# The way out in two halves, the gMLP half among the last latents, and 24 sums on GpSimd

## The chip, the cores and the metric

One core of a Trainium2 chip runs the whole layer. The metric is device time in microseconds, the median of the runs. Engines by the profile's names: PE is TensorE, DVE VectorE, ACT ScalarE, POOL GpSimd, SP SyncE (which issues DMAs).

## The reference

A residual layer on x of 1024 rows (tokens) by 1024 columns, float32: a half-step feed-forward network (FFN1), a mixer, FFN2, and a norm.

```python
x = x + 0.5 * swiglu(rmsnorm(x, ffn1_norm), w_gate1, w_up1, w_down1)      # hidden width 2816
h = rmsnorm(x, mix_norm) @ w_in      # u 512 | v 512 | c_q 256 | c_kv 128 | k_rope 32
y_a = gmlp_mixer(u, v, ...)          # gelu(u) * (masked 128x128 mix of rmsnorm(gelu(v)) + b): 512 wide
y_b = mla_mixer(c_q, c_kv, k_rope, ...)   # 8 heads, block-causal softmax attention: 8 * 64 = 512 wide
y = concatenate([rmsnorm(y_a, gmlp_out_norm), rmsnorm(y_b, mla_out_norm)])
x = x + y @ w_out                    # 1024 x 1024
x = x + 0.5 * swiglu(rmsnorm(x, ffn2_norm), w_gate2, w_up2, w_down2)
x = rmsnorm(x, final_norm)
```

`y @ w_out` can be taken as two products, `y_a`'s 512 columns by the first 512 rows of `w_out` and `y_b`'s by the other 512.

## The kernel before

All tensors are cut into 8 row tiles of 128 tokens. Every matmul operand is split into a high part (rounded on ScalarE or GpSimd) and a low part (the rest, by a subtraction), and a product is three matmuls: high by high, high by low, low by high.

The kernel is written as a list of steps. A step carries the work that ends in its matmuls, and `before(n, work)` puts the preparation (loads, splits, sums) n steps earlier. The list is recorded once without emitting anything, to place every tile in one SBUF ring and in the eight PSUM banks by its first and last use; then it is emitted, and a scheduler puts the instructions of each engine in a row. A tile that takes the place of another waits for the last reader of it.

The stages, in the order of the list:

- FFN1 (and FFN2 alike, tag a and b). Class `GateUp` takes gate and up weights in 11 blocks u of 256 columns. A block is loaded as two tiles `raw0`, `raw1` by four DMAs of 512 KB, and seen as quarters A11, A21, A12, A22, of which `sums` (line 443) makes S1 = A21 + A22, S2 = S1 − A11, S4 = A12 − S2 and S3 = A11 − A21 by `sum` (439), line 441, on VectorE. `split` (455 and 456) makes the high part on ScalarE and the low part on VectorE. Seven products of a block (24 matmuls each, line 468) follow. The first products, P1 and P2, of blocks 0 to 2 stand ahead of all others (`EARLY`), since they need no sums. Class `Down` then multiplies by the down weights and adds to x; its result goes to DRAM as `x1d`.
- The mixer. `v_tile`, `u_tile`, `mix_pair` and `gmlp_pair` make the gMLP's y_a; `gmlp_pair` writes each normalised row tile `ya` to DRAM as `yAd` (line 897). `latent_in` (a), `key_rope` (k), `latent_T` (c) and `latent_tile` (l) make queries, keys and values of a row tile; a latent tile is 18 matmuls (917 to 926), then squares, sums and reciprocal roots on VectorE in some 30 short operations, and the normalised `qn` and `kn`.
- Attention by items (head h, pair of query tiles pi). `head_T` (973) transposes `qn` and `kn` of one head and half of the tokens; `score_pair` (988 to 994) makes scores, their maximum on VectorE and p on ScalarE; `transposed_p` (1017, 291), `weighted` (1026, 1027) and `folded` (1038, 1040) follow some steps later. A string of letters (1082) sets in which order latents and the first five attention steps x0 to x4 alternate.
- The way out. `load_out` (from 1117) loads one block k of 128 rows of `w_out`, its high part `woh` by ScalarE (1123) and its low part `wol` by GpSimd (1124), all eight in the last steps of attention. `y_tile` reads `yAd` back, normalises y_b beside it and transposes the eight blocks of a row tile. `out_tile` (1149) multiplies by 48 matmuls (1157, 1158, 1160), adds x from `x1d` (1163), stores `x2d`, and norms and transposes the row for FFN2 (287 square, 271 power on GpSimd, 305 scaling, 300 transposes).
- FFN2, whose first weight blocks are loaded at steps named by `load_at`, and the final norm.

Of the kernel before, what the change touches and what calls it, by code (L numbers as in the profile page):

```python
# [234 lines left out]
def block(nc, x, positions, ffn1_norm, ffn1_w_gate, ffn1_w_up,  # L235
# [881 lines left out]
    def load_out(k):
        hi = tile_([P, D], f"woh{k}", F32R)
        lo = tile_([P, D], f"wol{k}", F32R)
        for e in range(2):  # L1120
            es = slice(e * 512, (e + 1) * 512)
            raw = load(tile_([P, 512], f"raw_wo{k}_{e}"), wov[:, k, es])
            nc.scalar.copy(hi[:, es], raw)
            nc.gpsimd.tensor_tensor(lo[:, es], raw, f(hi[:, es]), op=ALU.subtract)
        wo[k] = (hi, lo)
# [8 lines left out]
    def y_tile(t):  # L1134
        y = tile_([P, D], f"y{t}")
        load(y[:, 0:GW], yAd[rows(t), :])
        ysrc = mx["yB"][t // 4][:, t % 4].rearrange("p h d -> p (h d)")
        r = row_rstd(ysrc, y[:, GW:], f"yb{t}", GW)
        nc.vector.scalar_tensor_tensor(y[:, GW:], ysrc, r, mx["goB"], op0=ALU.mult, op1=ALU.mult)
        hv = transposed(y, f"y{t}")  # L1140
        yh = tile_([P, KD, P], f"yh{t}", F32R)
        yl = tile_([P, KD, P], f"yl{t}", F32R)
        for k in range(2):
            split(hv[k], yh[:, 4 * k:4 * k + 4, :], yl[:, 4 * k:4 * k + 4, :])
        mx["y", t] = (yh, yl)
# [3 lines left out]
    def out_tile(t):  # L1149
        x2 = row_tile(x1d[rows(t), :], f"x2_{t}")  # L1150
        yh, yl = mx["y", t]
        pe = [bank(f"wo{t}_{e}") for e in range(2)]
        for k in range(KD):
            wh, wl = wo[k]
            for e in range(2):
                es = slice(e * 512, (e + 1) * 512)
                mm(pe[e], yh[:, k, :], wh[:, es], start=k == 0, stop=False)  # L1157
                mm(pe[e], yh[:, k, :], wl[:, es], start=False, stop=False)  # L1158
            for e in range(2):
# [81 lines left out]
```

## Time and profile before

| | us |
|---|---|
| median of 3 runs | 1762.07 (1761.93 to 1762.74) |
| the profiled execution | 1762.42 |
| its span | 1760.6 |
| TensorE busy | 1716.5 (97%), 8196 instructions |
| VectorE busy | 1132.8 (64%) |
| ScalarE busy | 740.3 (42%) |
| GpSimd busy | 151.5 (9%) |

The busy share is an average over stages: TensorE is busy without a break in most of the two FFNs, and idle for some microseconds at a time elsewhere. A matmul counts as busy also while it runs at the lower clock, so the granted clock of a stretch is read beside its busy time.

### The profile page before, as it was taken

The numbers are of one execution on the slowest core, as the hardware profiler recorded it, in microseconds if no ns is written. First come the engines' busy times: TensorE is split into PE (matmuls) and PEld (weight loads), VectorE is DVE, ScalarE is ACT, GpSimd is POOL, SyncE is SP. The second block draws the span as 40 slices with busy tenths as digits, with TensorE's granted clock in tenths as the row PEclk, the third lists the DMA queues.
The fourth block names the chain that finished last, engine by engine and source line by source line (L and its number), as shares of the span: only waits on it lengthen the run. The fifth ranks groups of instructions, "written<-read, shape, count | busy, mean of one in ns | idle before, by whom it ended". The sixth has DMA issues, their size and how long they took to land.

```text
span 1760.6 us, 21281 instructions
## 1 busy us (share of the span) xinstructions
PE 1716.5 (97%) x8196; PEld 1446.7 (82%) x8196; DVE 1132.8 (64%) x1597; ACT 740.3 (42%) x1125; POOL 151.5 (9%) x288
## 2 busy tenths in 40 slices
PE   8999999999999999999799999999999999999997
PEld 7788888888888888898699888778888888888886
DVE  7965656555578567469777644675665555648774
ACT  6533333334324344346577823443333333433442
POOL 1100000000000004333200511000000000000010
PEclk9999999999999999999799999999999999999999
DMA  7043232325835521200000422413322231693431
GB/s 257 12 144 120 90 120 90 112 74 195 313 125 186 167 85 48 94 25 1 1 1 1 158 88 97 161 54 112 127 102 90 96 118 70 210 345 107 161 126 48
DMA packets 122981, 199.51 MB, mean 113 GB/s; under 512 B 11008, under 2 KB 57600, under 8 KB 122880
## 3 DMA queue, kind: packets, MB, share of 16 engines
q1 hardware_dynamic: 118784, 184.52, 31.1%
q0 software_dynamic: 3520, 12.58, 1.8%
q8 instruction: 64, 1.05, 0.2%
q10 hardware_dynamic: 576, 1.05, 0.2%
q14 instruction: 37, 0.30, 0.1%
HBM read 143.07 MB, written 55.05 MB: 113 GB/s over the span
## 4 chain that ended last, share of the span: by engine, by line
PE 90%; DVE 4%; ACT 3%; DMA 2%; issue 1%; POOL 0%; SPq 0%; POOLq 0%; ACTq 0%; DVEq 0%
PE psum L468 46%; PE psum L597 8%; PE psum L599 8%; PE psum L600 8%; PE psum L744 2%; PE psum L745 2%; PE psum L746 2%; PE psum L1160 2%; PE psum L1157 2%; PE psum L1158 2%; PE psum L1017 2%; PE psum L300 1%; PE psum L1027 1%; PE psum L1026 1%; PE psum L988 1%; PE psum L990 1%
## 5 line engine op out<-in xcount | busy, mean ns | idle before, releaser
L483 DVE TENSOR_TENSOR P_a<-psum,P_a 128x1024 f32<-128x1024 f32 x33 | 40.3, 1222 | 80.1 <-PE psum L468 80.1
L483 DVE TENSOR_TENSOR P_b<-psum,P_b 128x1024 f32<-128x1024 f32 x33 | 40.3, 1222 | 59.4 <-PE psum L468 59.4
L473 ACT COPY P_b<-psum 128x1024 f32<-128x1024 f32 x33 | 33.5, 1014 | 77.3 <-PE psum L468 77.3
L473 ACT COPY P_a<-psum 128x1024 f32<-128x1024 f32 x33 | 33.5, 1016 | 73.4 <-PE psum L468 73.4
L484 ACT ACTIVATE P_a<-P_a 128x512 f32<-128x512 f32 x33 | 20.9, 633 | 102.7 <-DVE P_a L483 102.6
L271 POOL TENSOR_TENSOR r_fin<-ms_fin,mhalf 128x1 f32<-128x1 f32 x8 | 7.0, 876 | 610.7 <-DVE ms_fin L269 610.7
L291 DVE TENSOR_TENSOR pl<-psum,ph 128x512 fp32r<-128x512 f32 (+1 forms) x80 | 48.5, 629 | 14.1 <-ACT ph L291 14.1
L992 DVE TENSOR_REDUCE nm<-psum 128x1 f32<-128x128 f32 (+3 forms) x64 | 47.0, 751 | 12.9 <-PE psum L990 12.8
L725 POOL DMA_DIRECT2D x1d<-x_a x8 | 4.6, 580 | 569.9 <-DVE x_a L611 568.3
L994 ACT ACTIVATE p<-psum,nm 128x128 f32<-128x128 f32 (+3 forms) x64 | 47.8, 752 | 12.9 <-DVE nm L992 11.7
L484 ACT ACTIVATE P_b<-P_b 128x512 f32<-128x512 f32 x33 | 20.8, 631 | 76.6 <-DVE P_b L483 76.4
L1157 PE MATMUL psum<-woh,yh 128*128 128x512 f32 x128 | 51.2, 400 | 0.0
L1158 PE MATMUL psum<-wol,yh 128*128 128x512 f32 x128 | 49.9, 390 | 0.0
L1017 PE MATMUL psum<-ident,p 128*128 128x128 f32 x288 | 44.2, 285 | 4.9 <-ACT p L994 4.9
L1027 PE MATMUL psum<-pl,vv 128*128 128x256 f32 x160 | 43.7, 299 | 3.2 <-DVE pl L291 3.2
L1160 PE MATMUL psum<-woh,yl 128*128 128x512 f32 x128 | 45.2, 392 | 0.0
L1026 PE MATMUL psum<-ph,vv 128*128 128x256 f32 x160 | 43.9, 298 | 1.3 <-ACT ph L291 1.3
L291 ACT CAST ph<-psum 128x512 fp32r<-128x512 f32 (+1 forms) x80 | 41.4, 559 | 8.5 <-PE psum L1017 6.6
L988 PE MATMUL psum<-kh,qh 128*128 128x512 f32 (+2 forms) x96 | 38.6, 406 | 3.7 <-ACT kn L940 3.5
L1017 PEld LDWEIGHTS psum<-ident,p 128*128 128x128 f32 x288 | 35.0, 148 | 7.7 <-ACT p L994 5.9
L611 DVE SCALAR_TENSOR_TENSOR x_b<-psum,x_b 128x512 f32<-128x512 f32 x32 | 21.0, 685 | 27.0 <-PE psum L600 27.0
L1027 PEld LDWEIGHTS psum<-pl,vv 128*128 128x128 f32 x160 | 31.3, 196 | 4.9 <-DVE pl L291 3.6
(525 smaller groups left out, 5256.9 us busy)
## 6 DMA issues: line engine op xcount, KB each, us to landing
raw_a<-in_ffn_w_gate SPq DMA_DIRECT2D x22, 512.0 KB, 4.3
raw_a<-in_ffn_w_up SPq DMA_DIRECT2D x22, 512.0 KB, 5.7
hd<-hS_a SPq DMA_DIRECT2D x44, 256.0 KB, 2.2
raw_b<-in_ffn_w_gate SPq DMA_DIRECT2D x22, 512.0 KB, 4.1
...
```

Source lines behind the costliest of these rows:

```text
L291: return nc.scalar.copy(hi, src), nc.vector.tensor_tensor(lo, src, f(hi), op=ALU.subtract)
L468: mm(bk[:, m * 512:(m + 1) * 512], lhs[:, 4 * m + k, :], rhs[:, k, :], start=pn in FIRST and n == k == 0, stop=n == 2 and k == 3, skip_gro ...
L473: nc.scalar.copy(ev[u, pn], bk)
L483: nc.vector.tensor_tensor(c, bk, c, op=ALU.add)
L597: mm(banks[t], hh[:, j, tl], dh[:, j, :], start=pn in DOWN_FIRST and c == 0 and j == 0, stop=False, skip_group_check=True)
L599: mm(banks[t], hh[:, j, tl], dl[:, j, :], start=False, stop=False, skip_group_check=True)
L600: mm(banks[t], hl[:, j, tl], dh[:, j, :], start=False, stop=c == 5, skip_group_check=True)
L1017: nc.tensor.transpose(ps[:, i * P:(i + 1) * P], prs[j][:, c * P:(c + 1) * P], ident)
L1027: mm(acc[:, 0:256], mx["vv"][c][:, h, :], lo, start=False, stop=i == len(pts) - 1)
L1157: mm(pe[e], yh[:, k, :], wh[:, es], start=k == 0, stop=False)
L1158: mm(pe[e], yh[:, k, :], wl[:, es], start=False, stop=False)
L1160: mm(pe[e], yl[:, k, :], wh[:, e * 512:(e + 1) * 512], start=False, stop=k == KD - 1)
```

## The change

Five edits, as the diff has them.

1. The way out is split by the rows of `w_out`. The normalised gMLP tiles `ya` stay in SBUF; `yAd` is gone. `load_out` of blocks 0 to 3 moves to the latents, and a new work `o` (`out_a`) takes one row tile's 24 matmuls of the gMLP half, adds x1 and stores x15 = x1 + y_a half to `x15d` by GpSimd's queue. The eight o-steps stand among the last latents and the first attention steps in the string of letters, each with its four transposes (`y_a`) a step earlier. At the end `out_tile` has the other 24 matmuls and adds to x15. The matmuls of a tile run high by high, high by low, low by high over all blocks, no longer block by block. Only `load_out` of blocks 4 to 7 is left in attention's last steps.
2. The string of letters also has another order of a, k, c and l, and only x0 to x2 in it; the attention's first rounds go over two heads where there were three, with `head_T` placed to match.
3. `sum` is on GpSimd for u < 3: 12 sums of 128x1024 in each FFN.
4. FFN2's weights of blocks 0 and 1 are loaded two steps earlier (block 1: one or two).
5. `y_tile` of tiles 2 to 7 stands two steps ahead of its out tile, not one.

Over the whole program GpSimd gets 24 sums of 128x1024 that VectorE had; VectorE gets 16 more additions of 128x512 (the gMLP half's). The number of matmuls and of ScalarE's instructions is the same.

```diff
@@ sum
-            nc.vector.tensor_tensor(t, self.value(u, x0), self.value(u, x1), op=op)
+            (nc.gpsimd if u < 3 else nc.vector).tensor_tensor(t, self.value(u, x0), self.value(u, x1), op=op)
@@ gmlp_pair
-            nc.gpsimd.dma_start(yAd[rows(t), :], ya)
+            mx["ya", t] = ya
@@ attention
-    items = [(h, pi) for ps in ((0, 1), (2, 3)) for h in range(3) for pi in ps]
-    items += [(h, pi) for h in range(3, H) for pi in range(NT // 2)]
+    items = [(h, pi) for ps in ((0, 1), (2, 3)) for h in range(2) for pi in ps]
+    items += [(h, pi) for h in range(2, H) for pi in range(NT // 2)]
...
-        if n == 2:
-            st.do(lambda: head_T(2, 0))
-        if n == 5:
+        if n == 3:
             st.do(lambda: head_T(0, 1))
             st.do(lambda: head_T(1, 1))
...
-                if op == "T" and n == 8:
-                    st.do(lambda: head_T(2, 1))
-                if op == "T" and 1 < h < H - 1 and pi in TP:
+                if op == "T" and 0 < h < H - 1 and pi in TP:
@@ the way out
+    def y_transposed(y, t, half):
+        ps = bank(f"ty{half}{t}")
+        for k in range(4):
+            nc.tensor.transpose(ps[:, k * P:(k + 1) * P], y[:, k * P:(k + 1) * P], ident)
+        yhl = tile_([P, 2, 4, P], f"yhl{half}{t}", F32R)
+        split(ps.rearrange("p (k t) -> p k t", k=4), yhl[:, 0], yhl[:, 1])
+        return yhl
+
+    def out_half(t, half, src):
+        xt = row_tile(src[rows(t), :], f"x{half}_{t}")
+        yhl = mx.pop(("yhl", half, t))
+        pe = [bank(f"wo{half}{t}_{e}") for e in range(2)]
+        for n, (i, j) in enumerate(((0, 0), (0, 1), (1, 0))):
+            for e in range(2):
+                for k in range(4):
+                    mm(pe[e], yhl[:, i, k, :], wo[4 * half + k][j][:, e * 512:(e + 1) * 512], start=n == k == 0,
+                       stop=n == 2 and k == 3)
+        for e in range(2):
+            es = slice(e * 512, (e + 1) * 512)
+            nc.vector.tensor_tensor(xt[:, es], pe[e], xt[:, es], op=ALU.add)
+        return xt
+
+    def out_a(t):
+        xt = out_half(t, 0, x1d)
+        nc.gpsimd.dma_start(x15d[rows(t), :], xt)
+
+    def y_a(t):
+        mx["yhl", 0, t] = y_transposed(mx.pop(("ya", t)), t, 0)
...
-    for ch in ("u0 u1 m0 g0 u2 u3 m1 g1 u4 u5 m2 g2 u6 u7 m3 g3 a0 c0 a1 k0 l0 c1 a2 l1 c2 a3 k1 l2 c3 a4 l3 c4 a5 k2 l4 "
-               "c5 a6 c6 a7 l5 c7 k3 x0 l6 x1 l7 x2 x3 x4").split():
+    for ch in ("u0 u1 m0 g0 u2 u3 m1 g1 u4 u5 m2 g2 u6 u7 m3 g3 a0 c0 a1 k0 l0 c1 a2 a3 k1 l1 c2 a4 a5 k2 l2 c3 a6 a7 k3 l3 c4 "
+               "o0 l4 c5 o1 l5 c6 o2 l6 c7 o3 l7 o4 x0 o5 o6 x1 o7 x2").split():
...
+    for t in range(NT):
+        sm[f"o{t}"].before(1, lambda t=t: y_a(t))
+    for k in range(4):
+        sm["o0"].before(8 - 2 * k, lambda k=k: load_out(k))
...
-    for k in range(KD):
-        att[last - 3 + k // 2].before(0, lambda k=k: load_out(k))
+    for k in range(4):
+        att[last - 2 + k // 2].before(0, lambda k=k: load_out(4 + k))
...
     def y_tile(t):
-        y = tile_([P, D], f"y{t}")
-        load(y[:, 0:GW], yAd[rows(t), :])
+        y = tile_([P, GW], f"y{t}")
...
+        mx["yhl", 1, t] = y_transposed(y, t, 1)
...
     def out_tile(t):
-        x2 = row_tile(x1d[rows(t), :], f"x2_{t}")
...
+        x2 = out_half(t, 1, x15d)
...
-        ws_[t].before(1, lambda t=t: y_tile(t), ws_[0].index)
+        ws_[t].before(2, lambda t=t: y_tile(t), ws_[0].index)
...
-    gu2.steps(GU_ORDER, base2 - 1, load_at={(0, 0): base2 - 2, (0, 1): base2 - 1, (1, 0): base2, (1, 1): base2,
+    gu2.steps(GU_ORDER, base2 - 1, load_at={(0, 0): base2 - 4, (0, 1): base2 - 3, (1, 0): base2 - 2, (1, 1): base2 - 1,
                                              (2, 0): base2, (2, 1): base2})
```

How the rows of an engine stand now, at three places. First TensorE where the last latents end: `chl6` is the transposed latent of row tile 6, `wuq`, `wkv` are its weights, `qn` and `kn` what the heads are transposed from. Before:

```order
L973 MATMUL psum_70<-ident_71,qn3_7165 128x128
L903 MATMUL psum_70<-ident_71,at1_6515 128x128 x3
L917 MATMUL psum_70<-wuq0h_6596,chl6_7409 128x384
L918 MATMUL psum_70<-wuq0l_6597,chl6_7409 128x384
L973 MATMUL psum_70<-ident_71,kn0_6785 128x128
L973 MATMUL psum_70<-ident_71,kn1_6909 128x128
L973 MATMUL psum_70<-ident_71,kn2_7043 128x128
L973 MATMUL psum_70<-ident_71,kn3_7168 128x128
L919 MATMUL psum_70<-wuq0h_6596,chl6_7409 128x384
L917 MATMUL psum_70<-wuq1h_6600,chl6_7409 128x384
L918 MATMUL psum_70<-wuq1l_6601,chl6_7409 128x384
L919 MATMUL psum_70<-wuq1h_6600,chl6_7409 128x384
```

After, behind the last six matmuls of latent 6:

```order
L924 MATMUL psum_70<-wkv_h_6599,chl6_7666 128x512
L925 MATMUL psum_70<-wkv_l_6600,chl6_7666 128x512
L926 MATMUL psum_70<-wkv_h_6599,chl6_7666 128x512
L924 MATMUL psum_70<-wkv_h_6599,chl6_7666 128x512
L925 MATMUL psum_70<-wkv_l_6600,chl6_7666 128x512
L926 MATMUL psum_70<-wkv_h_6599,chl6_7666 128x512
L1091 MATMUL psum_70<-ident_71,ya3_6373 128x128 x4
L1104 MATMUL psum_70<-woh0_7102,yhl02_7659 128x512
L1104 MATMUL psum_70<-woh1_7196,yhl02_7659 128x512
L1104 MATMUL psum_70<-woh2_7263,yhl02_7659 128x512
L1104 MATMUL psum_70<-woh3_7329,yhl02_7659 128x512
L1104 MATMUL psum_70<-wol0_7104,yhl02_7659 128x512
```

Where the kernel before went from a latent to the first head's transposes (`kn0` to `kn3`, of tiles 0 to 3) and back, the gMLP tile 3's transposes and the out tile 2's matmuls stand now.

Second, ScalarE ahead of p of head 6, row tile 6 (`p6_6`), with the copies of `w_out`'s blocks (`woh`). Before:

```order
L1123 CAST woh0_9735<-raw_wo0_0_9739 128x512
L1123 CAST woh0_9735<-raw_wo0_1_9743 128x512
L977 ACTIVATE qh7_9625<-psum_70,gqcol_95 128x512
L1123 CAST woh1_9749<-raw_wo1_0_9752 128x512
L1123 CAST woh1_9749<-raw_wo1_1_9758 128x512
L1123 CAST woh3_9849<-raw_wo3_0_9854 128x512
L977 ACTIVATE kh7_9629<-psum_70,gkcol_96 128x512
L1123 CAST woh2_9836<-raw_wo2_0_9840 128x512
L1123 CAST woh2_9836<-raw_wo2_1_9844 128x512
L1123 CAST woh3_9849<-raw_wo3_1_9858 128x512
L994 ACTIVATE p6_6_9691,rs6_3_9680<-psum_70,nm6_6_9687 128x896
```

After:

```order
L1083 CAST woh4_10166<-raw_wo4_0_10171 128x512
L1083 CAST woh4_10166<-raw_wo4_1_10176 128x512
L1083 CAST woh5_10181<-raw_wo5_0_10186 128x512
L977 ACTIVATE kh7_9988<-psum_70,gkcol_96 128x512
L1083 CAST woh5_10181<-raw_wo5_1_10191 128x512
L994 ACTIVATE p6_6_10049,rs6_3_10039<-psum_70,nm6_6_10046 128x896
L1029 COPY oT6_1_10084<-psum_70 128x256
L1083 CAST woh6_10282<-raw_wo6_0_10287 128x512
```

Eight copies of half a block stood ahead of `p6_6`; four stand there now, of blocks 4 and 5 alone.

Third, GpSimd at the start of FFN1, from the head gains (`gkcol`) on; `inv`, `posf` and `ang` belong to the rotary tables. Before:

```order
L699 TENSOR_SCALAR gqcol_95<-graw_644 64x1
L700 COPY gkcol_96<-graw_644 64x1
L704 MEMSET inv_651 128x1 x16
L706 CAST posf_669<-pos_91 128x8
L708 TENSOR_TENSOR ang_673<-posf_669,inv_651 128x128
L725 DMA x1d_86<-x_a0_3905 128x1024
```

After:

```order
L699 TENSOR_SCALAR gqcol_95<-graw_644 64x1
L700 COPY gkcol_96<-graw_644 64x1
L441 TENSOR_TENSOR S1_a0_555<-raw0_a0_117,raw1_a0_121 128x1024
L441 TENSOR_TENSOR S2_a0_558<-S1_a0_555,raw0_a0_117 128x1024
L441 TENSOR_TENSOR S4_a0_591<-raw1_a0_121,S2_a0_558 128x1024
L441 TENSOR_TENSOR S3_a0_594<-raw0_a0_117 128x1024
L704 MEMSET inv_651 128x1 x16
L706 CAST posf_669<-pos_91 128x8
L708 TENSOR_TENSOR ang_673<-posf_669,inv_651 128x128
L441 TENSOR_TENSOR S1_a1_846<-raw0_a1_320,raw1_a1_325 128x1024
L441 TENSOR_TENSOR S3_a1_885<-raw0_a1_320 128x1024
L441 TENSOR_TENSOR S2_a1_850<-S1_a1_846,raw0_a1_320 128x1024
L441 TENSOR_TENSOR S4_a1_882<-raw1_a1_325,S2_a1_850 128x1024
```

The first block's four sums stand between `gkcol` and the rotary tables, the second block's four behind these.

## Rows read from the trace of the kernel before

**Rows 1.** Stretches of the span (us): busy time (instructions) by engine, granted clock, DMA.

```profile
core 0: us, PE busy (x) PEld busy (x) DVE busy (x) ACT busy (x) POOL busy (x), PEclk, DMA share, GB/s
...
35.00:100.00 65.00, 62.46 (x278) 50.35 (x277) 57.41 (x75) 31.28 (x39) 8.03 (x20) 1.00 0.15 53
...
800.00:880.00 80.00, 65.59 (x351) 59.02 (x350) 65.06 (x196) 47.41 (x110) 24.91 (x55) 0.81 0.00 1
880.00:975.00 95.00, 93.67 (x702) 87.88 (x701) 74.28 (x143) 68.92 (x160) 6.94 (x38) 1.00 0.03 9
975.00:1000.00 25.00, 21.61 (x148) 20.07 (x147) 15.51 (x31) 22.97 (x53) 21.39 (x25) 0.93 0.50 159
1000.00:1110.00 110.00, 109.92 (x582) 93.32 (x581) 54.72 (x96) 41.54 (x85) 12.55 (x23) 1.00 0.32 108
1110.00:1170.00 60.00, 54.63 (x234) 44.45 (x233) 44.39 (x45) 28.59 (x33) 1.14 (x2) 0.94 0.30 101
```

**Rows 2.** TensorE's waits, 800–880 us: line, who ended them, sum, times, longest.

```profile
PE psum L973 <- DVE chl L291: 3.8, 1, 3.8
PE psum L988 <- ACT kn L940: 3.5, 1, 3.5
PE psum L1027 <- DVE pl L291: 3.0, 2, 2.6
```

**Rows 3.** TensorE's waits, 975–1170 us.

```profile
PE psum L468 <- ACT A11h_b L455: 3.4, 1, 3.4
PE psum L1017 <- ACT p L994: 3.2, 1, 3.2
PE psum L468 <- DVE P_b L483: 1.9, 1, 1.9
```

**Rows 4.** TensorE's timeline in the out stage: start, us, line, operation.

```profile
1043.65 0.39 PE L1157 MATMUL psum<-woh,yh 128*128 128x512 f32 x1
1043.87 0.39 PE L1158 MATMUL psum<-wol,yh 128*128 128x512 f32 x1
...
1046.37 1.04 PE L300 MATMUL psum<-ident,xn_f 128*128 128x128 f32 x8
1047.24 0.60 PE L300 MATMUL psum<-ident,y 128*128 128x128 f32 x4
```

**Rows 5.** Groups of instructions, 1020–1110 us: count | busy, mean ns | idle before.

```profile
L1163 DVE TENSOR_TENSOR x<-psum,x 128x512 f32<-128x512 f32 x14 | 9.1, 685 | 6.6 <-PE psum L1160 5.6 <-DMA x<-x1d 1.1
L305 DVE SCALAR_TENSOR_TENSOR xn_f<-x,r_f,g 128x1024 f32<-128x1024 f32 x7 | 9.0, 1285 | 5.2 <-POOL r_f L271 5.2
L291 DVE TENSOR_TENSOR yl<-psum,yh 128x512 fp32r<-128x512 f32 x12 | 8.1, 682 | 0.0
L287 ACT ACTIVATE xn_f<-x 128x1024 f32<-128x1024 f32 x7 | 7.4, 1061 | 12.0 <-DVE x L1163 9.8 <-issue 2.1
...
L271 POOL TENSOR_TENSOR r_f<-ms_f,mhalf 128x1 f32<-128x1 f32 x7 | 3.9, 559 | 4.9 <-DVE ms_f L269 4.9
```

**Rows 6.** GpSimd's groups over the whole span.

```profile
L1124 POOL TENSOR_TENSOR wol<-raw_wo,woh 128x512 fp32r<-128x512 f32 x16 | 20.2, 1312 | 1.7 <-ACT woh L1123 1.7
```

**Rows 7.** ScalarE's timeline at the end of attention.

```profile
977.63 1.20 ACT L1123 CAST woh<-raw_wo 128x512 fp32r<-128x512 f32 x2
...
982.09 1.64 ACT L1123 CAST woh<-raw_wo 128x512 fp32r<-128x512 f32 x3
983.64 1.00 ACT L994 ACTIVATE p<-psum,nm 128x896 f32<-128x896 f32 x1
```

**Rows 8.** SyncE's DMA queue before FFN2.

```profile
1109.18 0.37 SPq L311 DMA_DIRECT2D raw_b<-in_ffn_w_gate  x1
...
1115.52 1.32 SPq L311 DMA_DIRECT2D raw_b<-in_ffn_w_up  x1
```

**Rows 9.** ScalarE's timeline at the start of FFN2.

```profile
1125.98 1.04 ACT L455 CAST A11h_b<-raw_b 128x1024 fp32r<-128x1024 f32 x1 [0.34 <-DMA raw_b<-in_ffn_w_up]
```

**Rows 10.** Line 441 over the whole span: ns min/median/max.

```profile
L441 DVE TENSOR_TENSOR S_a<-raw_a,raw_a x11: 1211/1219/1226, 41.5 to 388.9; 128x1024 f32<-128x1024 f32 x11
```

**Rows 11.** GpSimd's timeline in the first 20 us.

```profile
13.85 1.04 POOL L455 CAST A11h_a<-raw_a 128x1024 fp32r<-128x1024 f32 x1
```

**Rows 12.** VectorE's timeline in the first 20 us.

```profile
13.93 2.04 DVE L305 SCALAR_TENSOR_TENSOR xn_f<-xa,r_f,g 128x1024 f32<-128x1024 f32 x1
```

**Rows 13.** GpSimd's timeline at the start of FFN1.

```profile
37.03 1.65 POOL L700 COPY gkcol<-graw 64x1 f32<-64x1 f32 x1 [0.37 <-DMA graw<-in_k_head_norm]
47.97 0.54 POOL L704 MEMSET inv<- 128x1 f32 x16 [9.29 <-DVE S_a L441]
```

More of the change, by code (lines that the diff above doesn't have):

```diff
@@ L636, in block @@
     x2d = nc.dram([S, D], "x2d")
-    yAd = nc.dram([S, GW], "yAd")
+    x15d = nc.dram([S, D], "x15d")
     hds = [nc.dram([7 * NU * P, 512], f"hd{i}") for i in range(2)]
@@ L1076, in attend, with load_out @@
                 st.do(lambda i=items[n - D1]: weighted(*i))
+    wov = w_out[0].rearrange("(k p) e -> p k e", p=P)
+    wo = {}
+    def load_out(k):
+        hi = tile_([P, D], f"woh{k}", F32R)
+        lo = tile_([P, D], f"wol{k}", F32R)
+        for e in range(2):
+            es = slice(e * 512, (e + 1) * 512)
+            raw = load(tile_([P, 512], f"raw_wo{k}_{e}"), wov[:, k, es])
+            nc.scalar.copy(hi[:, es], raw)
+            nc.gpsimd.tensor_tensor(lo[:, es], raw, f(hi[:, es]), op=ALU.subtract)
+        wo[k] = (hi, lo)
@@ new lines, in y_transposed @@
+    def y_transposed(y, t, half):
[14 more added lines that the diff above has]
+                       stop=n == 2 and k == 3)
+        for e in range(2):
+            es = slice(e * 512, (e + 1) * 512)
+            nc.vector.tensor_tensor(xt[:, es], pe[e], xt[:, es], op=ALU.add)
+        return xt
@@ L1079, in block @@
+    def out_a(t):
[3 more added lines that the diff above has]
+        mx["yhl", 0, t] = y_transposed(mx.pop(("ya", t)), t, 0)
     vs = [Step(lambda t=t: v_tile(t)) for t in range(NT)]
     sm = {}
-    works = {"u": u_tile, "m": mix_pair, "g": gmlp_pair, "a": latent_in, "k": key_rope, "c": latent_T, "l": latent_tile}
-    for ch in ("u0 u1 m0 g0 u2 u3 m1 g1 u4 u5 m2 g2 u6 u7 m3 g3 a0 c0 a1 k0 l0 c1 a2 l1 c2 a3 k1 l2 c3 a4 l3 c4 a5 k2 l4 "
-               "c5 a6 c6 a7 l5 c7 k3 x0 l6 x1 l7 x2 x3 x4").split():
+    works = {"u": u_tile, "m": mix_pair, "g": gmlp_pair, "a": latent_in, "k": key_rope, "c": latent_T, "l": latent_tile, "o": out_a}
@@ L1112, in block @@
         attend(n)
-    wov = w_out[0].rearrange("(k p) e -> p k e", p=P)
-    wo = {}
     last = len(items) - 1
[L1117 to L1125, printed above, removed]
-    for k in range(KD):
-        att[last - 3 + k // 2].before(0, lambda k=k: load_out(k))
+    for k in range(4):
+        att[last - 2 + k // 2].before(0, lambda k=k: load_out(4 + k))
     def out_gain_b():
@@ L1134, in y_tile @@
     def y_tile(t):
-        y = tile_([P, D], f"y{t}")
-        load(y[:, 0:GW], yAd[rows(t), :])
+        y = tile_([P, GW], f"y{t}")
         ysrc = mx["yB"][t // 4][:, t % 4].rearrange("p h d -> p (h d)")
[L1138 to L1145, printed above, removed]
+        r = row_rstd(ysrc, y, f"yb{t}", GW)
+        nc.vector.scalar_tensor_tensor(y, ysrc, r, mx["goB"], op0=ALU.mult, op1=ALU.mult)
+        mx["yhl", 1, t] = y_transposed(y, t, 1)
     xo2 = XOps("f2")
     def out_tile(t):
-        x2 = row_tile(x1d[rows(t), :], f"x2_{t}")
[L1151 to L1159, printed above, removed]
-                mm(pe[e], yl[:, k, :], wh[:, e * 512:(e + 1) * 512], start=False, stop=k == KD - 1)
-        for e in range(2):
-            es = slice(e * 512, (e + 1) * 512)
-            nc.vector.tensor_tensor(x2[:, es], pe[e], x2[:, es], op=ALU.add)
+        x2 = out_half(t, 1, x15d)
         nc.gpsimd.dma_start(x2d[rows(t), :], x2)
```

## The prediction

> **What bounds the kernel now.** First the table of stretches [rows 1]: in each, TensorE's busy time against the length, and the clock it was granted. What a stretch loses is its length less busy time × granted clock. From 100 to 760 us and from 1170 to 1715 us nothing is lost, so nothing that the change does there can count. The losses lie in four places: 800–880, (80 − 65.59) + 65.59 × 0.19 = 14.4 + 12.5 = 26.9 us; 1110–1170, 5.4 + 3.3 = 8.7; 975–1000, 3.4 + 1.5 = 4.9; 35–100, 2.5. The clock term is no cause of its own: in those stretches it falls to the lower of its two levels (1.2 of 2.4 GHz) around the holes, and 880–975, whose holes sum to 1.3 us, kept 1.00. So a hole that goes takes about as much again with it.
>
> Second, who ended those holes. In 800–880, where the last latent tiles alternate with the first scores, the longest three waited for VectorE's and ScalarE's work on latent tiles [rows 2], with VectorE busy 65.06 of 80 us. At 981 TensorE waits for a softmax tile p, at 1124 for the first quarter of an FFN2 weight block, at 1157 for VectorE [rows 3].
>
> **The sum, by parts.** It is made against the profiled execution (1762.42 us); the median of the three runs, 1762.07, is 0.35 lower, taken off at the end. Matmuls and transposes are the same in number (8132), so TensorE gains only where it waits.
>
> (a) *The gMLP half among the latents.* 8 tiles × 24 matmuls start 0.22–0.23 us apart [rows 4]: 43.7 us, and 32 transposes at 0.87 for eight [rows 4] make 47.2. They leave 1000–1110, where nothing waited, for a place with holes. TensorE's own work in 800–880 at full clock is 65.59 × 0.81 = 53.1 us; with the new work 100.3. VectorE's is 65.06, plus 16 evictions of 0.685 [rows 5], plus 8 splits of about the same, 81.5; GpSimd's 8 low halves of the weights, 1.31 each [rows 6], could hold it back by another 10.5, 92.0 at most. So TensorE becomes the longer of the two. A loaded VectorE need not stall TensorE: at 57.41 of 65 us (35–100) 2.5 us were lost, at 74.28 of 95 only 1.3 [rows 1]. By that alone 24 of the 26.9 could go. Against it stands the new order: latents 4, 5 and 6 follow each other with nothing between, though each needs ScalarE's copies of the one before; the out tiles' banks wait for VectorE's evictions, which queue behind the latents' norm chains; and the first heads' transposes still wait for the last latent. I count three or four holes of the size in [rows 2], as many as now, but with TensorE busy for longer between. I leave half: **−13.5** (−4 to −24).
>
> (b) *End of attention.* ScalarE made eight half-copies of weights between 977.63 and 983.64, just ahead of the p for which TensorE waited 3.2 us [rows 3, 7]; now four stand there. Copies start (983.64 − 982.09) / 3 = 0.52 apart, so p comes 4 × 0.52 = 2.1 earlier, and with the dip of 1.5: **−3.6** (−1 to −4.9).
>
> (c) *Start of FFN2.* The hole of 3.4 at 1124 [rows 3] ended with a copy of raw weights at 1125.98, which a load had released; such loads were issued from 1109.18 to 1115.52 in a row, with a row tile of x among them [rows 8, 9]. They now start two steps earlier. If SyncE's queue still holds them for a free buffer, nothing is won. The second hole, 1.9, waits for VectorE; 8 sums leave it here, 8 × 1.22 = 9.8 us [rows 10], and if GpSimd's 8 × 2.6 (below) blocked it wholly it would have 44.39 − 9.8 + 20.8 = 55.4 of 60 us, still room. I let the long hole and most of the dip go, and keep the second hole and 0.8 of dip: 8.7 − 2.7 = **−6** (−8.7 to 0).
>
> (d) *The out stage at half its matmuls.* A tile gives TensorE 24 × 0.228 = 5.5 us where it gave 48 × 0.228 = 10.9, and the transposes of the normalised row wait behind two evictions (1.4), the square (1.06), its mean, GpSimd's power (0.56) and the scaling (1.285) [rows 5]: 4.3, with hand-overs 5. Before, a cover of 10.9 hid that; now the order puts some transposes in the middle of the next tile's matmuls. Three to four holes near 1.2: **+5** (0 to 8 × 1.2 = +9.6). The rest of that tile (x15 instead of x1 read, y's gMLP half not read) goes to queues with room: DMA share 0.32 there [rows 1].
>
> (e) *Start of FFN1, sums on GpSimd.* No row shows a 128x1024 sum on GpSimd. The nearest is the 128x512 subtraction, 1.31 [rows 6]: twice that is 2.6; below it, VectorE's own 1.22 [rows 10]; above, twice GpSimd's 1.31 again if it must also wait for VectorE each time, 5.2. I take 2.6, since operation and engine are the same. That it isn't GpSimd's time alone the trace shows at 13.9: beside a GpSimd copy from 13.85 on, VectorE's scaling with two operands in SBUF took 2.04 instead of 1.285 [rows 5, 11, 12]. So count each such sum as time that VectorE cannot use: of the eight sums of blocks 0 and 1 in 35–100, 8 × 2.6 = 20.8 come and 9.8 go: 57.41 + 11.0 = 68.4 of 65 us, **+3.5**. If no operation of VectorE were blocked it would have 47.6, and the 2.5 lost there would vanish: −2.5. If block 2's four sums also fell there (+5.5) with a dip of the clock like that of 1110–1170, +10. GpSimd's other work there isn't urgent, though the first sum stands behind the copy that ends at 38.7 [rows 13].
>
> The page "GPSIMD Engine Reference" of the Trainium skill (section 4.1, Engine selection) speaks against this part: elementwise work belongs on VectorE, GpSimd being about half as fast with two inputs; its section 3.1 has 4497 ns for twice our width, an estimate of 2.25 us for a sum. The ratio agrees with 2.6 against 1.22. With 2.25 part (e) would come to +0.6.
>
> Sum: −13.5 − 3.6 − 6 + 5 + 3.5 = −14.6; 1762.4 − 14.6 = 1747.8, less 0.35, **1747.5 us**.
>
> **Rivals.**
> R1, *slower: the sums on GpSimd decide*. While GpSimd and VectorE take turns, each 2.6 us sum delays VectorE one for one, and the four sums of a block, each built on the one before, run late for products of that block. Price: (e) at its end, +10, and (c) turned from −6 to +8.5 (eight sums at a net 1.4, 11.2, and a dip of 3.3): −13.5 − 3.6 + 8.5 + 5 + 10 = +6.4, 1768.5. It decides from the point where both FFN starts together cost over 15.6 us (12.1 that the other parts win, and 3.5). For it: [rows 11, 12], and that most of VectorE's work there takes two operands from SBUF. Against it: VectorE's slack at FFN2, 15.6 of 60 us [rows 1]. The page "SBUF — State Buffer" (the Trainium skill, "Who interferes with whom") states this as a rule: one of the two holds the shared ports for a whole instruction and the other blocks fully. The 0.75 us extra at 13.93 agrees with it.
>
> R2, *VectorE's chains bound the latents*: the out tiles only fill what is then waited for elsewhere, (a) = −4: 1757. For it: all three long holes end on VectorE or ScalarE. Against: 880–975, with as loaded a VectorE, lost next to nothing.
>
> R3, *full fill*: (a) at −24 and no holes in the out stage: −24 − 3.6 − 6 + 0 + 3.5 = −30, 1732. For it: 47 us of work that waits for nothing. Against: the order of latents 4 to 6.
>
> R4, *the tail doesn't do what it says*: the loads are held back by buffers, (c) = 0, and the shorter out tiles cost +9.6: 1758.
>
> **How the numbers follow.** Forecast 0.45 (1740 to 1753), R3 0.15, R2 0.14, R4 0.12, R1 0.10, and 0.04 for a mix that cancels. A difference of 0.2%, 3.5 us, is about what a measurement here can tell from none: faster means under 1758.5, slower over 1765.6. Forecast, R3 and most of R2 and R4 are faster, 0.80; the rest of those two and the mix, 0.10, the same; R1, 0.10, slower. The range takes in all but R1 and the lower end of R3: 1730 to 1762.
>
> **What would show it.** In the profile after: stretch of the latents with out tiles at a granted clock over 0.9 and under 14 us lost (a); p at the end of attention no longer waited for over 1.5 us (b); no hole over 2 us on raw weights at FFN2 (c); holes of about 1 us between out tiles, on xn (d); GpSimd sums of 2.2 to 3 us, VectorE's operations beside them longer by up to that, and block 0 of FFN1 done some 3.5 us later (e). The prediction is wrong if the sums take 4 us or more, if the clock stays at its lower level through the latents although they are filled, or if the attention starts later because its first heads come behind the out tiles.

## The result, and the profile after

| | before | after |
|---|---|---|
| median, us | 1762.40 (1761.93 to 1765.33, 4 runs) | 1747.88 (1747.24 to 1751.6, 4 runs) |
| the profiled execution / its span | 1762.42 / 1760.6 | 1748.02 / 1746.2 |
| VectorE busy, instructions | 1132.8, 1597 | 1139.7, 1589 |
| GpSimd busy, instructions | 151.5, 288 | 216.7, 312 |

The ratio is 0.9919, with a 95% interval of 0.9901 to 0.9936: 14.5 us faster, where 14.6 were forecast. That agreement is partly luck: the terms behind it were off by some 2 to 3.5 us each, in both directions.

The stretches of the span after, with the columns of [rows 1]; the latents lie from 770 to 875, the out stage from 1053 to 1107:

```profile
core 0: us, PE busy (x) PEld busy (x) DVE busy (x) ACT busy (x) POOL busy (x), PEclk, DMA share, GB/s
...
35.00:110.00 75.00, 69.18 (x297) 56.19 (x296) 63.02 (x68) 33.34 (x41) 34.23 (x31) 0.95 0.19 60
...
800.00:880.00 80.00, 75.30 (x373) 64.30 (x372) 62.70 (x199) 37.97 (x88) 37.38 (x62) 0.98 0.30 102
880.00:975.00 95.00, 92.88 (x661) 85.12 (x661) 72.09 (x146) 64.09 (x151) 11.08 (x43) 1.00 0.06 21
975.00:1020.00 45.00, 43.13 (x324) 40.36 (x323) 35.25 (x69) 34.32 (x80) 8.24 (x28) 1.00 0.12 37
1020.00:1095.00 75.00, 67.17 (x394) 57.67 (x392) 47.75 (x91) 40.91 (x94) 16.31 (x25) 0.98 0.45 146
1095.00:1170.00 75.00, 75.00 (x351) 62.45 (x350) 63.82 (x60) 39.46 (x49) 25.56 (x14) 1.00 0.24 83
```

In 800–880 the clock is 0.98 where it was 0.81, and TensorE is busy 75.3 of 80 us where it was 65.6. The start of FFN2 (1107 on) has no hole left. New losses stand in 35–110 (5.8 of 75 us idle, clock 0.95) and in 1020–1095 (7.8 idle). TensorE's waits, first from the latents to the end of attention, then in the out stage:

```profile
PE psum L1104 <- DVE x L1108: 3.3, 2, 2.0
PE psum L1017 <- ACT p L994: 3.2, 5, 1.3
PE psum L917 <- ACT kn L940: 1.3, 1, 1.3
PE psum L1027 <- DVE pl L291: 1.2, 2, 0.6
```

```profile
PE psum L1104 <- ACT b_f L376: 4.6, 2, 2.3
PE psum L1104 <- ACT yhl L291: 1.7, 1, 1.7
```

The holes of 3.8, 3.5 and 2.6 of [rows 2] have become holes of at most 2.0; p at the end of attention is waited for 1.3 at most, not 3.2 [rows 3]. The out tiles, which lost 0.7 in all before, wait up to 2.3 each, two of them for a bank (`b_f`, a copy out of it) and one for its transposed y (`yhl`).

To add this up for all kernels alike, take the time between the starts of each two successive matmuls, less what that size takes where nothing waits (0.227 us for 512 columns [rows 4]; 0.190, 0.174, 0.119 and 0.109 for 416, 384, 256 and 128), and sum it over a stage. This *loss* holds holes and low clock together. FFN1's stretch is from its first product to 100 us, FFN2's its first 80 us. Worked out from the profiled executions, beside the medians (e3's and e7's profiled executions were 3 to 4 us faster than their medians):

| us lost | FFN1 start | latents, attention | out stage | FFN2 start | FFN2 end | median |
|---|---|---|---|---|---|---|
| before | 7.7 | 37.5 | 0.7 | 9.2 | 1.5 | 1762.4 |
| after | 13.3 | 19.5 | 9.2 | 0.1 | 0.1 | 1747.9 |
| e1, all sums on VectorE | 7.7 | 19.2 | 11.0 | 0.4 | 0.1 | 1744.3 |
| e2, GpSimd sums in FFN2 alone | 7.7 | 19.3 | 12.9 | 3.6 | 0.1 | 1750.0 |
| e3, loads late | 12.3 | 16.8 | 10.8 | 6.8 | 0.1 | 1756.0 |
| e4, no split | 12.3 | 41.6 | 0.7 | 9.6 | 1.5 | 1772.4 |
| e5, e1 with b_f on VectorE | 7.7 | 19.7 | 6.1 | 0.1 | 0.1 | 1739.6 |
| e6, e1 bank by bank | 9.1 | 22.1 | 9.4 | 0.1 | 0.1 | 1747.7 |
| e7, e1 with FFN2 products early | 7.8 | 18.7 | 5.7 | 3.1 | 1.5 | 1746.7 |
| e8, before with GpSimd sums | 12.3 | 35.5 | 0.7 | 12.6 | 1.5 | 1769.5 |
| e9, e1 with three heads | 9.1 | 41.9 | 10.8 | 0.1 | 0.1 | 1768.7 |
| e10, e1 with late sums on GpSimd | 7.7 | 18.0 | 9.4 | 0.4 | 0.1 | 1743.6 |
| e11, e5 with b_f first | 9.1 | 16.6 | 12.6 | 0.1 | 0.1 | 1745.1 |
| e12, e5 with the last tile late | 7.8 | 21.6 | 6.4 | 7.8 | 1.5 | 1749.5 |

After less before, from unrounded values: +5.5 − 18.0 + 8.5 − 9.1 − 1.5 = −14.6, against a span 14.4 shorter. Each row is one execution. Kernels whose FFN1 is written alike differ there by 1.0 to 1.4 (7.7 to 9.1 without sums on GpSimd, 12.3 to 13.3 with them), so a difference of 1 or 2 in a column says little.

### The profile page after: what moved, and what is told of

Its sections match the earlier page's. It is cut to its first block, busy times and chain, and to the rows that moved or that the text cites. A ratio compares the mean times of both kernels' runs of the same rounds, so it can differ in the third digit from the quotient of the medians.

```text
span 1746.2 us, 21337 instructions
## 1 busy us (share of the span) xinstructions
PE 1709.4 (98%) x8196; PEld 1440.0 (82%) x8196; DVE 1139.7 (65%) x1589; ACT 739.1 (42%) x1125; POOL 216.7 (12%) x312
## 4 chain that ended last, share of the span: by engine, by line
PE 90%; DVE 4%; ACT 2%; DMA 1%; issue 1%; POOL 1%; SPq 0%; POOLq 0%; ACTq 0%; DVEq 0%
PE psum L468 46%; PE psum L600 8%; PE psum L597 8%; PE psum L599 8%; PE psum L1104 4%; PE psum L744 2%; PE psum L746 2%; PE psum L745 2%; PE psum L1017 2%; PE psum L1027 1%; PE psum L1026 1%; PE psum L988 1%; PE psum L990 1%; PE psum L989 1%; PE psum L300 1%
## 5 line engine op out<-in xcount | busy, mean ns | idle before, releaser
L1104 PE MATMUL psum<-woh,yhl 128*128 128x512 f32 x256 | 69.8, 404 | 9.7 <-ACT b_f L376 4.6
L1104 PEld LDWEIGHTS psum<-woh,yhl 128*128 128x128 f32 x256 | 48.0, 193 | 21.5 <-ACT b_f L376 5.1
L992 DVE TENSOR_REDUCE nm<-psum 128x1 f32<-128x128 f32 (+3 forms) x64 | 47.0, 751 | 10.3 <-PE psum L990 10.2
L994 ACT ACTIVATE p<-psum,nm 128x128 f32<-128x128 f32 (+4 forms) x64 | 47.7, 751 | 12.9 <-DVE nm L992 7.5
L1104 PE MATMUL psum<-wol,yhl 128*128 128x512 f32 x128 | 36.6, 407 | 0.0
L485 DVE TENSOR_TENSOR hA_b<-P_b 128x512 f32<-128x512 f32 x33 | 26.3, 798 | 12.7 <-ACT P_b L484 12.7
```

What stands on the lines that cost most here:

```text
L1104: mm(pe[e], yhl[:, i, k, :], wo[4 * half + k][j][:, e * 512:(e + 1) * 512], start=n == k == 0, stop=n == 2 and k == 3)
```

## The experiments

### The sums on GpSimd

How the two engines meet at the start of FFN1, after: GpSimd's timeline, then VectorE's.

```profile
38.76 2.40 POOL L441 TENSOR_TENSOR S_a<-raw_a,raw_a 128x1024 f32<-128x1024 f32 x1
41.24 3.26 POOL L441 TENSOR_TENSOR S_a<-S_a,raw_a 128x1024 f32<-128x1024 f32 x1
44.58 2.71 POOL L441 TENSOR_TENSOR S_a<-raw_a,S_a 128x1024 f32<-128x1024 f32 x1
```

```profile
39.20 3.05 DVE L456 TENSOR_TENSOR A12l_a<-raw_a,A12h_a 128x1024 fp32r<-128x1024 f32 x1
42.17 2.88 DVE L388 TENSOR_TENSOR xT2l_f<-bT_f,xT2h_f 128x512 fp32r<-128x512 f32 x1
44.98 0.68 DVE L386 TENSOR_TENSOR bT_f<-psum,b_f 128x512 f32<-128x512 f32 x1
45.58 2.26 DVE L388 TENSOR_TENSOR xT2l_f<-bT_f,xT2h_f 128x512 fp32r<-128x512 f32 x1
```

The low half at 39.20 took 3.05 us where the same line took 1.21 at 36.9: it got through only when the sum of 38.76 was done. The next sum, 3.26 instead of 2.40, waited in turn for it. So the two take turns one for one. The page "SBUF — State Buffer" of the Trainium skill (Who interferes with whom) has the lock behind this: whoever issues first has the shared ports for a whole instruction, and the other blocks fully. The trace agrees, with five waits of 0.3 to 2.2 us in these lines. The addition at 44.98, with one operand in PSUM, kept its 0.68.

TensorE pays for it at 69.98, where it waits for the eviction P_a, which stands behind the delayed operations on VectorE. Its other waits in 35–110 are 1.2 and 0.9; before, the longest in 35–100 was 1.2:

```profile
PE psum L468 <- DVE P_a L483: 3.7, 1, 3.7
```

**e1: all sums on VectorE**

```diff
-            (nc.gpsimd if u < 3 else nc.vector).tensor_tensor(t, ...
+            nc.vector.tensor_tensor(t, ...
```

> The changed kernel with all 24 sums on VectorE again, nothing else undone. Theory: on GpSimd they cost 5.5 us at the start of FFN1 (TensorE's loss up to 100 us went from 7.7 to 13.3) and win nothing at FFN2, whose start gained 9.1 by the earlier loads: FFN1's loss back at 7.7, FFN2's first 80 us still under 1 us lost, 1742.4. Rival: at FFN2 the sums on GpSimd took the hole of 1.9 us that waited for VectorE, with its dip of the clock: that hole returns, 3 to 4 us, 1745.5 to 1746.5.

Measured 1744.26 (1742.55 to 1744.55), ratio to before 0.9896 (0.9881 to 0.9912). FFN1's loss is back at 7.7 exactly, and FFN2's start stays at 0.4: the rival falls. The sums on GpSimd gave nothing in either place. That the time fell by 3.6, not 5.5, is the out stage, 1.8 worse in another order that the scheduler made. The intervals of the two ratios overlap, so the gain of 3.6 rests on the FFN1 column of the traces: 7.7 to 9.1 in all kernels without these sums, 12.3 to 13.3 in the four with them.

**e2: GpSimd's sums in FFN2 alone**

```diff
-            (nc.gpsimd if u < 3 else nc.vector).tensor_tensor(t, ...
+            (nc.gpsimd if u < 3 and self.tag == "b" else nc.vector).tensor_tensor(t, ...
```

> The changed kernel with GpSimd's sums in FFN2 alone, FFN1's twelve on VectorE. Both theories: FFN1's loss up to 100 us back from 13.3 to 7.7, 1742.4. It differs from the kernel with all sums on VectorE by what GpSimd's sums give at FFN2 alone: 0 by the theory that the loads did it, 3 to 4 us less time here by the rival. If instead the loss at FFN1 stays near 13, the shared access of the two engines was not its cause.

Measured 1750.01 (1745.99 to 1751.04): FFN1 is back at 7.7, but 5.7 us slower than e1, a result that neither theory had. VectorE and GpSimd at the start of FFN2 in e2:

```profile
1118.01 5.09 DVE L388 TENSOR_TENSOR xT2l_f<-bT_f,xT2h_f 128x512 fp32r<-128x512 f32 x2
1123.03 6.75 DVE L407 TENSOR_TENSOR b_f<-b_f,bT_f 128x1024 f32<-128x1024 f32 x2
```

```profile
1117.07 2.68 POOL L441 TENSOR_TENSOR S_b<-raw_b 128x1024 f32<-128x1024 f32 x1 [7.13 <-ACT bB_f L389]
...
1125.43 3.25 POOL L441 TENSOR_TENSOR S_b<-raw_b,S_b 128x1024 f32<-128x1024 f32 x1
```

```profile
PE psum L468 <- DVE P_b L483: 3.2, 1, 3.2
```

Two splits took 5.09 us, two differences 6.75 (each 2.35 a pair or less in e1), and the eviction P_b behind them came 3.2 us late for TensorE. Of the 5.7, 3.2 are lost here and 1.9 in the out stage. In the changed kernel the same four sums cost nothing; its rows there stand otherwise. So the price is real also at FFN2, but hangs on the order.

**e8: the kernel before with GpSimd's sums**

```diff
-            nc.vector.tensor_tensor(t, ...
+            (nc.gpsimd if u < 3 else nc.vector).tensor_tensor(t, ...
```

> The kernel before with nothing changed but the 24 sums on GpSimd. Theory (VectorE's operations on two operands in SBUF and GpSimd's sums shut each other out, nothing is won): FFN1's start loses 4.6 to 5.5 more, FFN2's start 0 to 5 more than 9.2: 1767 to 1773, VectorE's operations beside a sum up to 2.4 us longer each. Rival (they relieve VectorE at FFN2, where TensorE waited for it): FFN2's start loses 3 to 4 less, 1763 to 1764.

Measured 1769.46 (1766.51 to 1771.95), ratio 1.0041 (1.0028 to 1.0054): +4.6 at FFN1, +3.4 at FFN2. By itself this part of the change makes the kernel slower; the rival falls.

**e10: the sums of the last three blocks on GpSimd**

```diff
-            nc.vector.tensor_tensor(t, ...
+            (nc.gpsimd if u >= 8 else nc.vector).tensor_tensor(t, ...
```

> The same kernel (1744.3) with the sums of each FFN's last three blocks on GpSimd, as many as the change put there, but where VectorE has idle time. Theory: the two engines still shut each other out there (sums of 2.4 to 3.6 us, VectorE's operations beside them up to 2.4 longer), but TensorE waits for none of it: 1743 to 1746. Rival: such a sum costs wherever it stands, as at the start of FFN1 some 0.4 us each: 1749 to 1755.

Measured 1743.64 (1742.0 to 1747.18), no difference from e1. Line 441 in e10, ns min/median/max:

```profile
L441 POOL TENSOR_TENSOR S_a<-raw_a,raw_a x3: 2396/2407/2875, 310.8 to 389.6; 128x1024 f32<-128x1024 f32 x3
L441 POOL TENSOR_TENSOR S_a<-S_a,raw_a x3: 2389/2396/2721, 313.3 to 395.7; 128x1024 f32<-128x1024 f32 x3
```

Some sums still are held (2875 against 2396), so the two still meet, and TensorE waits for none of it. The price is a matter of the place.

### The loads of FFN2

**e3: weights loaded as before**

```diff
-... load_at={(0, 0): base2 - 4, (0, 1): base2 - 3, (1, 0): base2 - 2, (1, 1): base2 - 1,
+... load_at={(0, 0): base2 - 2, (0, 1): base2 - 1, (1, 0): base2, (1, 1): base2,
```

> The changed kernel with FFN2's first weight blocks loaded at the steps of the kernel before. Theory: the hole of 3.4 us on the first quarter's copy returns, with its dip of the clock, 5 to 7 us lost in FFN2's first 80 us: 1753 to 1755. Rival, that the shorter way out and the sums on GpSimd opened that start: under 2 us lost there, 1748 to 1750.

Measured 1755.99 (1752.63 to 1757.72), with 6.8 us lost at the start of FFN2. The size is the theory's, the mechanism isn't. TensorE's only wait there, and ScalarE's copy P_b with what VectorE and GpSimd did ahead of it:

```profile
PE psum L468 <- ACT P_b L473: 4.2, 1, 4.2
```

```profile
1159.88 1.01 ACT L473 COPY P_b<-psum 128x1024 f32<-128x1024 f32 x1 [4.70 <-DVE xT4l_f L397]
```

```profile
1154.27 5.52 DVE L397 TENSOR_TENSOR xT4l_f<-b_f,xT4h_f 128x1024 fp32r<-128x1024 f32 x2 [1.12 <-ACT xT4h_f L396]
```

```profile
1152.03 3.40 POOL L441 TENSOR_TENSOR S_b<-raw_b 128x1024 f32<-128x1024 f32 x1
1155.39 3.32 POOL L441 TENSOR_TENSOR S_b<-S_b,raw_b 128x1024 f32<-128x1024 f32 x1
```

No wait on raw weights came back. The late loads shifted the second block's sums on GpSimd to where VectorE makes xT4's low half: 5.52 us instead of 2.35. So undoing the early loads alone costs 6.7 at this place, but e3 does not show that they closed the hole of [rows 3]; late loads with the sums on VectorE would tell, and were not tried.

### The latents

**e4: no split** (the kernel before with the new letters less the o's, two-head rounds and GpSimd's sums)

```diff
-    items = [... for h in range(3) for pi in ps]
+    items = [... for h in range(2) for pi in ps]
-... a2 l1 c2 a3 k1 l2 c3 a4 l3 c4 a5 k2 l4 c5 a6 c6 a7 l5 c7 k3 x0 l6 x1 l7 x2 x3 x4
+... a2 a3 k1 l1 c2 a4 a5 k2 l2 c3 a6 a7 k3 l3 c4 l4 c5 l5 c6 l6 c7 l7 x0 x1 x2
```

> The kernel before with the new order of the latents (without out tiles), the two-head rounds of attention and the sums on GpSimd, but the way out whole at the end, and the loads where they were, since all of w_out leaves no room for them earlier. Theory: what the latents gained, they gained by the out tiles' matmuls between them: TensorE's loss from the latents to the end of attention stays at 37 us or above, the sums cost 5.5, FFN2's start keeps its 9: 1768 to 1776. Rival: the new order of latents and heads gained it: loss there about 20 us, 1750 to 1753.

Measured 1772.42 (1771.57 to 1773.03), 41.6 us lost from the latents to the end of attention: the new order without the out tiles is 4 worse than the old. TensorE waits 12.3 us in one piece for the first head's kh:

```profile
PE psum L988 <- ACT kh L977: 12.3, 1, 12.3
```

**e9: three heads** (e1 with the rounds and the `head_T` of the kernel before; the o's stay)

```diff
-    items = [... for h in range(2) for pi in ps]
-    items += [(h, pi) for h in range(2, H) for pi in range(NT // 2)]
+    items = [... for h in range(3) for pi in ps]
+    items += [(h, pi) for h in range(3, H) for pi in range(NT // 2)]
```

> The kernel with all sums on VectorE (measured 1744.3, 19.2 us lost from the latents to the end of attention) with the attention's first rounds over three heads again, and head_T where the kernel before had it. Theory: the out tiles' matmuls took the loss there from 37 to 19, not the rounds: 17 to 21 us lost, 1742 to 1746. Rival: with two heads the first scores ask VectorE for less at the busiest time, and that is a part of the gain: 23 to 28 lost, 1748 to 1753.

Measured 1768.71 (1765.81 to 1769.87): 24 us slower than e1, and the theory that the out tiles alone did it falls, and so does the size of the rival. TensorE, ScalarE, GpSimd and SyncE in e9:

```profile
826.02 3.78 PE L1108 MATMUL psum<-woh,yhl 128*128 128x512 f32 x8 [10.33 <-ACT yhl L291]
```

```profile
825.38 0.59 ACT L291 CAST yhl<-psum 128x512 fp32r<-128x512 f32 x1 [6.84 <-POOL late L820]
```

```profile
814.86 4.99 POOL L1088 TENSOR_TENSOR wol<-raw_wo,woh 128x512 fp32r<-128x512 f32 x4 [3.03 <-ACT woh L1087]
```

```profile
782.20 30.07 SPq L311 DMA_DIRECT2D raw_wo<-in_w_out  x8
```

The out tile waited 10.3 us for its own transposed y (`yhl`), whose split waited for GpSimd's last use of a rotary tile (`late`), whose place in the ring it takes. GpSimd came late to that since four low halves of w_out had run in one piece just before. They were late since of the eight loads of w_out, each waiting for the last reader of its place, three were out by 789 us and the fourth only at 806.7; in e1 six were out by 797.6. The work is the same, the places are others. That three heads' q and k fill the ring is inferred, not shown. The letters stayed those made for two heads, so e9 is not the old order with out tiles in it; that kernel was not run.

### The out stage

**e5: the copies b_f on VectorE** (e1, FFN2's rows alone)

```diff
-            nc.scalar.copy(self.b[key][:, :, cs], v)
+            (nc.vector.tensor_copy if self.nm == "f2" else nc.scalar.copy)(self.b[key][:, :, cs], v)
```

> The kernel with all sums on VectorE (measured 1744.3, 11.0 us lost in the out stage), with the copies b_f of the transposed rows, which free the banks that the next out tile's matmuls wait for, on VectorE instead of ScalarE, for FFN2's rows alone. Theory: those banks are held because the copies stand behind the next row's square in ScalarE's queue; without that the three holes of 5.4 us in all on b_f fall under 2, the loss there to 5 to 7, 1739 to 1741. Rival, as the prediction had it: the chain of eviction, square, mean, power and scaling is itself longer than a tile's 6.8 us of TensorE work, the holes move to the transposes of xn, loss 10 to 12, 1743 to 1746.

Measured 1739.59 (1737.44 to 1740.13), ratio to before 0.9874 (0.9856 to 0.9892): the fastest kernel of the study, ahead of both. The loss fell from 11.0 to 6.1 as expected. First one of the holes in e1: ScalarE ahead of it, then TensorE.

```profile
1054.38 1.07 ACT L287 ACTIVATE xn_f<-x 128x1024 f32<-128x1024 f32 x1
...
1055.90 1.09 ACT L376 COPY b_f<-psum 128x512 f32<-128x512 f32 x2
```

```profile
1056.55 1.84 PE L1104 MATMUL psum<-woh,yhl 128*128 128x512 f32 x4 [2.28 <-ACT b_f L376]
```

The square of the next row (L287) stands ahead of the copies. So it does at the other hole of 2.3; at the third, of 0.8, no square stands between. Then VectorE and TensorE around one tile in e5:

```profile
1063.07 0.69 DVE L291 TENSOR_TENSOR xB11l_f<-psum,xB11h_f 128x512 fp32r<-128x512 f32 x1 [0.36 <-ACT xB11h_f L291]
1063.68 0.68 DVE L376 COPY b_f<-psum 128x512 f32<-128x512 f32 x1
```

```profile
PE psum L1104 <- DVE ms_f L269: 3.6, 3, 1.2
PE psum L1104 <- DVE b_f L376: 1.2, 1, 1.2
```

Four holes of 1.2 are left where there were three of 2.3, 0.8 and 2.3 on the copies and two smaller ones (1.4 and 0.9): the bank is free when the low half and the copy are done. At this tile the copy ends at 1064.36 and the matmuls start at 1064.51; `ms_f`, to which the profile puts three of the waits down, is the short operation next behind the copy on VectorE.

**e6: bank by bank**

```diff
-        for n, (i, j) in enumerate(((0, 0), (0, 1), (1, 0))):
-            for e in range(2):
+        for e in range(2):
+            for n, (i, j) in enumerate(((0, 0), (0, 1), (1, 0))):
```

> The same kernel (1744.3) with each out tile's 24 matmuls done bank by bank, twelve into the first and then twelve into the second, in both halves of the way out. By the theory of held banks the second bank is asked for 2.7 us later and the first half is evicted 2.7 us earlier: loss in the out stage from 11.0 to 4 to 6, 1738 to 1740, and among the latents no loss more than now (19). By the rival of the long chain the earlier eviction helps by at most 1.4: 1742 to 1744.

Measured 1747.68 (1746.21 to 1748.84): both expectations missed. Two holes of 2.3 on b_f remain, and each stands ahead of a tile's first matmul, so it is the tile's first bank that is held, which this edit doesn't touch; and 4.3 us more went elsewhere in another order. One of these losses is at the end of attention, where TensorE waits 3.1 for p again. ScalarE there:

```profile
1016.51 0.62 ACT L1083 CAST woh<-raw_wo 128x512 fp32r<-128x512 f32 x1 [2.74 <-DMA raw_wo<-in_w_out]
1017.04 1.11 ACT L994 ACTIVATE p<-psum,nm 128x1024 f32<-128x1024 f32 x1
```

The copy of a weight block stood ahead of p and waited 2.74 us for its load. So a copy that takes 0.5 us can hold p for much longer.

**e11: the copy ahead of the split** (e5, FFN2's rows alone)

```diff
-... for op in (self.cut, self.keep)]
+... for op in ((self.keep, self.cut) if self.nm == "f2" else (self.cut, self.keep))]
```

> The kernel with the copies b_f on VectorE (measured 1739.6, 6.1 us lost in the out stage by four holes of 1.4), with each copy ahead of the split of the same bank. Theory: the bank is then free after the split's two operations alone, 0.7 us earlier: holes of 0.7, 3 to 4 us lost there, 1736.5 to 1738. Rival: what holds the tile is the whole chain of casts, and the other order of the queue puts a hole elsewhere: 6 or more lost, 1739 to 1742.

Measured 1745.14 (1744.35 to 1747.73). The rival: the transposes of two rows now come within 5 us of each other, and TensorE waits for the scaled row,

```profile
PE psum L300 <- DVE xn_f L305: 7.2, 2, 3.6
```

two holes of 3.6. Here the long chain of the prediction's step (d) is seen.

**e7 and e12: out tiles within FFN2's first steps** (e1 with tiles 6 and 7 moved; e5 with tile 7)

```diff
+    LATE = ((6, 0), (7, 1))        # e12: ((7, 0),)
+    for t, j in LATE:
+        steps[base2 + j].before(2, lambda t=t: y_tile(t), ws_[0].index)
+        steps[base2 + j].do(lambda t=t: out_tile(t))
```

> The same kernel (1744.3) with the last two out tiles done within the first two steps of FFN2, whose first products need only the row tiles 0 to 3, and its weights loaded at steps -2, -1, 0, 0, 2, 2 against that start (earlier leaves no room). If the out stage is too thin, products of 5.4 us between its last tiles take 3 to 5 of the 11.0 lost: 1739 to 1741. Rival: weights that come later bring back a hole as in the kernel with late loads (6 to 7 us): 1747 to 1750.

> The kernel with the copies b_f on VectorE (1739.6) with the last out tile done within FFN2's first step, and that FFN's weights loaded at steps -3, -2, -1, 0, 1, 1 against its start. Theory: products of FFN2 between the last tiles fill 1 to 2 of the 6.1 us lost: 1737.5 to 1739. Rival: later weights or sums make TensorE wait at FFN2's start, 2 us or more lost there: 1741 or above.

Measured 1746.65 (1742.66 to 1747.74) and 1749.53 (1747.8 to 1751.44), against 1744.3 and 1739.6 without. In e7 the out stage, now of six tiles, lost 5.7 in place of 11.0, but FFN2's start 3.1 and its end 1.5. That adds up to some 2 us less than e1, and the profiled execution, the fastest of four, was 1.6 faster than e1's median; the other three took 3.2 to 5.1 longer than that one, and no trace shows where. So it is open whether e7 gains or loses. In e12 the out stage lost 6.4, no less than e5's 6.1, and FFN2's start 7.8, with TensorE waiting 2.0 and 1.9 for evictions P_b there. That the later weights brought these waits is not shown.

## Why the prediction was right, point by point

- *Where the time is lost* held: the four places of [rows 1] and the out stage moved, each with a term of the sum, but for 1.5 at the end of FFN2 (a wait of 1.2 for a split of down weights, wT4h_b, and its dip), which had none. It stands in the kernel before, e4, e7, e8 and e12 and in no other, and why is open. (The count of 8132 matmuls is not the profile's, which has 8196 before and after; no term uses it.)
- *(a) and (b)*, −17.1 forecast, −18.0 measured. The holes got shorter and the clock stayed up, as said. By the same count the last 45 us of attention lost 6.5 before and 4.5 after, so (a) won 16.0 where 13.5 was forecast and (b) 1.9 where 3.6 was. (b) is within what the order alone shifts: with the same four copies that stretch lost 7.2 in e5 and 8.9 in e6, where a copy waits for its load. (b) priced the copies' length and left out that wait. In (a) the missing term is edit 2: the two-head rounds have none, and the new order of the latents stands only among the reasons to halve. The new order and rounds without the out tiles (e4) lost 41.6, the out tiles in that order with three heads (e9) 41.9, against 37.5 before; all together win 18. Filling a wait needs the filler's own operands in time, and these need room. Which part of the win is the order of the letters is open, since no run had the out tiles in the old one.
- *(c)*, −6 forecast, −9.1 measured, just past its end of −8.7: the second hole went too. That the early loads did it by closing the hole on raw weights was argued and isn't shown: e3, without them, loses 6.7 more here, but that hole stayed away. [rows 9] already spoke against the step: the load takes 0.34 us of ScalarE's wait there, and just ahead of it ScalarE waited 1.65 for VectorE and then squared the last out tile's row:

```profile
1124.48 1.06 ACT L287 ACTIVATE xn_f<-x 128x1024 f32<-128x1024 f32 x1 [1.65 <-DVE x L1163]
```

In that order of ScalarE's rows, weights that come earlier give back 0.34 us of the hole, and more only if the row of x, for whose load VectorE waited 1.55, comes earlier with them. That the early loads find no room beside the whole way out is said in e4's expectation, and no run shows it.
- *(d)*, +5 forecast, +8.5 measured, within its range. The step that failed is the hole's size and cause: two holes of 2.3 and one of 1.7, not three or four of 1.2, and the two wait for a PSUM bank that ScalarE's copies free, not for the scaled row. e5 shows the cause in e1: with these copies on VectorE 4.9 of the loss went.
- *(e)*, +3.5 forecast, +5.5 measured (+4.6 in e3, e4 and e8, which have the same sums); e1 gives it back to the tenth. A sum takes 2.40 us alone, where 2.6 had been taken, and one of 24 took 4.44. (The estimate of 2.25 from section 3.1 of the page "GPSIMD Engine Reference" of the Trainium skill lies 0.15 below, a little nearer; the measurement decides.) So the term was not too small for the sums' length. The blocked operations stand ahead of an eviction that TensorE waits for (3.7), and the hole took the clock with it: granted 0.95 in 35–110, where it was 1.00.
- *Rivals.* R1's mechanism is there, as the rows above show, and decides in e8 (slower) and in most of e2's gap; its price in the changed kernel was 5.5, not the 18.5 that R1 asked for. The room at FFN2's start in [rows 1] does not explain that by itself, since e2 pays 3.2 there. R2's and R3's ends were both far off; of R4, the cost of the out tiles came (8.5 of 9.6) and the loss of (c) didn't.
- *Signs of being wrong.* One came true: attention starts later, behind the out tiles (first scores at 874.8, where it was 829.3), and the forecast held even so. It was a bad sign, since TensorE is busy with the out tiles meanwhile and they are gone from the end. The holes between out tiles on the scaled row, which were to show (d), did not come.

The best version here is e5: the split and the early loads, all sums on VectorE, and the copies that free the banks on VectorE, 1.3% under the kernel before.
